# Fifteen small loads queued behind the last store of a biased softmax

## The chip, the cores and the metric

The kernel runs on one core of one Trainium2 chip. The metric is the device time of one execution in microseconds (us), as the median over runs; the profile's span is the time from the first to the last instruction of one profiled execution.

## What is computed

For logits of shape (2, 8, 2112, 2112) and a table of 33 bias values for each of 8 heads, each logit gets the bias of its relative position, clipped to 16 on both sides, and each row of 2112 then goes through a softmax:

```python
rel = pos[:, None] - pos[None, :]
rel_clipped = np.clip(rel, -16, 16) + 16
logits = logits + rel_bias[:, rel_clipped][None]
exp = np.exp(logits - logits.max(axis=-1, keepdims=True))
return exp / exp.sum(axis=-1, keepdims=True)
```

All of it is in fp32. 285 MB are read and 285 MB written.

## The kernel before

The 33,792 rows are dealt to the 128 partitions, 264 consecutive rows (`ROWS`) to each. They are worked on in 44 chunks of 6 rows in each partition (`R`, `N`), in four buffers `X0` to `X3` of 50,688 bytes in each partition (`NBUF`). A chunk is loaded whole (128 partitions x 6 rows, 6,336 KB), changed in place and stored from the same buffer.

The order of the work is written out by hand, with semaphores and without a planner:

- SP issues every load and store of `X`. `load` (line 78) loads a chunk and counts on `ld[b]`; `store` (line 82) waits until DVE has scaled the rows and counts on `st[b]`. The first chunk is loaded as six single rows (line 88). Then a loop (line 204) stores a chunk, waits until an older store has landed, and loads the next chunk into that buffer. After the loop the last chunks are stored without further loads; the very last one goes out as two halves of three rows.
- `take` (line 74) makes an engine wait until a semaphore has reached a number and subtracts it again. SP's program ends with four of these, one for each buffer's stores.
- ACT loads the bias table once, to all partitions (line 97), and does the exponentials with their row sums (line 175).
- DVE builds a strip of bias values from the table in its first microseconds, and then copies it (line 160), adds it to the logits with the row's extremum (line 166), takes reciprocals of the sums (line 183), and scales the rows (line 187).
- GpSimd makes two small tables of indices.

Of the kernel before, what the change touches and what calls it, by code (L numbers as in the profile page):

```python
# [7 lines left out]
FP32 = mybir.dt.float32  # L8
# [7 lines left out]
def kernel(  # L16
# [6 lines left out]
    nc = tc.nc  # L23
    P = 128
# [3 lines left out]
    W = 2 * MR + 1  # L28
# [13 lines left out]
    io = ctx.enter_context(tc.tile_pool(name="io", bufs=1))  # L42
# [4 lines left out]
    tot = io.tile([P, STEP], FP32, tag="tot", name="tot")  # L47
    rec = io.tile([P, STEP], FP32, tag="rec", name="rec")
    ip = io.tile([P, 3, PB], I32, tag="ip", name="ip")
    ps = ctx.enter_context(tc.tile_pool(name="ps", bufs=1, space=bass.MemoryType.PSUM))  # L50
    M = ps.tile([P, 4096], FP32, tag="M", name="M")

    def view(t, offset, dims):

        return bass.AP(tensor=t.tensor, offset=t.offset + offset, ap=[[list(t.ap[0])[0], P]] + dims)

    def rows(t, j, n):

        return bass.AP(tensor=t.tensor, offset=t.offset + j * S, ap=[[ROWS * S, P], [1, n * S]])

    with tc.tile_critical(no_gpsimd_drain=True):
# [6 lines left out]
        rb = nc.alloc_semaphore("rb")  # L68
        pre = nc.alloc_semaphore("pre")
        idx = nc.alloc_semaphore("idx")  # L70
        dve = nc.alloc_semaphore("dve")

        def take(eng, sem, n):
            eng.wait_ge(sem, n).then_inc(sem, -n)  # L74
# [5 lines left out]
        def store(j, b, s0=0, n=R):  # L80
            take(nc.sync, scaled, n)
            nc.sync.dma_start(
                out=rows(out, j + s0, n), in_=X[b][:, s0 * S : (s0 + n) * S]
            ).then_inc(st[b], 16)


        for r in range(R):
            nc.sync.dma_start(
                out=X[0][:, r * S : (r + 1) * S], in_=rows(logits, r, 1)
            ).then_inc(ld[0] if r == R - 1 else pre, 16)  # L90
        for n in range(1, NBUF):
# [6 lines left out]
            out=rbB,  # L98
            in_=bass.AP(tensor=rel_bias.tensor, offset=rel_bias.offset, ap=[[0, P], [1, H * W]]),
# [27 lines left out]
        for m, op in ((eq, ALU.is_equal), (gt, ALU.is_gt), (le, ALU.is_le), (lt, ALU.is_lt)):  # L127
# [4 lines left out]
            out=view(F, 0, [[W, H], [1, W]]), in0=view(F, 0, [[W, H], [1, W]]),  # L132
# [9 lines left out]
            out=view(F, 0, [[W, PB], [1, W]]), in0=view(F, SC + 2 * PB, [[1, PB], [0, W]]),  # L142
# [7 lines left out]
            out=view(M, U, [[ROWS, PB], [1, W]]), in0=view(F, 0, [[W, PB], [1, W]]),  # L150
            in1=view(F, SC + 8 * PB, [[1, PB], [0, W]]), op=ALU.add))
        then(v.tensor_copy(out=view(M, U + W, [[ROWS, PB], [1, ROWS - W]]),  # L152
                           in_=view(F, SC + 7 * PB, [[1, PB], [0, ROWS - W]])))
# [56 lines left out]
            store(n * R, n % NBUF)  # L210
        store((N - 1) * R, (N - 1) % NBUF, 0, HALF)
        store((N - 1) * R, (N - 1) % NBUF, HALF, R - HALF)
        for b in range(NBUF):
            take(nc.sync, st[b], 32 if b == (N - 1) % NBUF else 16)

# [29 lines left out]
```

## Time and profile before

| what | us |
|---|---|
| time, median of 3 runs (1330.96 to 1332.85) | 1331.0 |
| span of the profiled execution | 1327.7 |
| time of the median outside the span | 3.3 |
| DVE busy | 976.6 |
| ACT busy | 575.2 |
| one load of a chunk, from issue to landing (median) | 44.6 |
| one store of a chunk, from issue to landing (median) | 52.6 |

The profiled execution's own time outside its span isn't recorded apart, so the span is set against the median of the runs. In the page, DVE is the vector engine, ACT the scalar engine, POOL is GpSimd, and SP the sync engine, which here only issues DMAs and waits. A `q` behind an engine's name stands for its sequencer. "DMA" in a window is the mean busy share of the core's 16 DMA engines; q1 is the queue that SP issues on and q10 the one that ACT issues on. Instructions that only issue a DMA or wait aren't counted as busy.

### The profile page before, as it was taken

The numbers are of one execution on the slowest core, as the hardware profiler recorded it, in microseconds if no ns is written. First come the engines' busy times: TensorE is split into PE (matmuls) and PEld (weight loads), VectorE is DVE, ScalarE is ACT, GpSimd is POOL, SyncE is SP. The second block draws the span as 40 slices with busy tenths as digits, with TensorE's granted clock in tenths as the row PEclk, the third lists the DMA queues.
The fourth block names the chain that finished last, engine by engine and source line by source line (L and its number), as shares of the span: only waits on it lengthen the run. The fifth ranks groups of instructions, "written<-read, shape, count | busy, mean of one in ns | idle before, by whom it ended". The sixth has DMA issues, their size and how long they took to land. (4 is left out here: it accounts for less than half of the span.)

```text
span 1327.7 us, 2454 instructions
## 1 busy us (share of the span) xinstructions
DVE 976.6 (74%) x911; ACT 575.2 (43%) x539; POOL 0.4 (0%) x6
## 2 busy tenths in 40 slices
DVE  6999667777777776687778777677877776687772
ACT  2564333444444343345444333444444343335440
POOL 0000000000000000000000000000000000000000
DMA  9999999999999999999999999999999999999998
GB/s 392 431 428 437 435 420 437 435 434 425 435 437 434 428 435 434 435 429 429 438 438 432 426 438 437 437 425 437 437 437 425 435 440 437 428 432 438 437 426 359
DMA packets 13683, 571.11 MB, mean 430 GB/s; under 512 B 1521, under 2 KB 1649, under 8 KB 1649
## 3 DMA queue, kind: packets, MB, share of 16 engines
q1 hardware_dynamic: 13536, 570.96, 99.6%
q10 hardware_dynamic: 144, 0.14, 0.1%
q14 instruction: 3, 0.02, 0.0%
HBM read 285.61 MB, written 285.47 MB: 430 GB/s over the span
## 5 line engine op out<-in xcount | busy, mean ns | idle before, releaser
L166 DVE CUSTOM_DVE_ANT_0 X<-X,F 128x2112 f32<-128x2112 f32 x264 | 605.2, 2354 | 301.3 <-DVEq L74 301.3
L175 ACT ACTIVATE X<-X,nmax 128x2112 f32<-128x2112 f32 x264 | 541.7, 2052 | 539.3 <-ACTq L74 517.6
L187 DVE TENSOR_SCALAR X<-X,rec 128x2112 f32<-128x2112 f32 x264 | 332.4, 1315 | 13.2
L175 ACT ACT_TABLE_LOAD x11 | 14.1, 1283 | 183.3 <-ACTq L74 183.3
L175 ACT ACTIVATION_READ_ACCUMULATOR X<-X,nmax 128x1 f32 x264 | 49.2, 186 | 0.0
L160 DVE COPY F<-M 128x2135 f32 x11 | 26.1, 2374 | 6.3 <-DVEq L74 6.3
L166 DVE DVE_READ_ACCUMULATOR2_ANT nmax<- 128x1 f32 x264 | 21.7, 82 | 0.0
L183 DVE RECIPROCAL rec<-tot 128x3 f32<-128x3 f32 x88 | 14.9, 170 | 0.0
L131 DVE TENSOR_TENSOR F<-F 128x264 f32<-128x264 f32 x1 | 0.4, 434 | 4.7 <-DMA F<-in_rel_bias_dram 4.7
L152 DVE COPY M<-F 128x1848 f32<-128x1848 f32 x1 | 2.1, 2077 | 0.0
L118 DVE TENSOR_SCALAR ip<-ip 128x8 int32<-128x8 int32 x1 | 0.2, 173 | 1.3 <-POOL ip L102 1.3
L135 DVE TENSOR_REDUCE rbS<-F 128x33 f32<-128x264 f32 x1 | 0.6, 610 | 0.0
L149 DVE TENSOR_TENSOR M<-F 128x264 f32<-128x264 f32 x1 | 0.4, 441 | 0.0
L141 DVE TENSOR_TENSOR F<-F,rbS 128x264 f32<-128x264 f32 x1 | 0.4, 425 | 0.0
L128 DVE TENSOR_SCALAR F<-F 128x8 f32<-128x8 f32 x4 | 0.4, 166 | 0.0
L154 DVE COPY M<-rbS 128x247 f32<-128x247 f32 x1 | 0.4, 408 | 0.0
L139 DVE TENSOR_SCALAR F<-F,rbS 128x8 f32<-128x8 f32 x1 | 0.2, 231 | 0.0
L145 DVE SCALAR_TENSOR_TENSOR F<-F,rbS 128x8 f32<-128x8 f32 x1 | 0.2, 225 | 0.0
L140 DVE TENSOR_SCALAR F<-F,rbS 128x8 f32<-128x8 f32 x1 | 0.2, 222 | 0.0
L146 DVE SCALAR_TENSOR_TENSOR F<-F,rbS 128x8 f32<-128x8 f32 x1 | 0.2, 219 | 0.0
L124 DVE TENSOR_TENSOR F<-ip 128x8 f32<-128x8 int32 x1 | 0.2, 167 | 0.0
L121 DVE TENSOR_TENSOR F<-ip 128x8 f32<-128x8 int32 x1 | 0.2, 166 | 0.0
(9 smaller groups left out, 1.2 us busy)
## 6 DMA issues: line engine op xcount, KB each, us to landing
X<-in_logits_dram SPq DMA_DIRECT2D x43, 6336.0 KB, 44.6
out_dram<-X SPq DMA_DIRECT2D x43, 6336.0 KB, 52.6
X<-in_logits_dram SPq DMA_DIRECT2D x6, 1056.0 KB, 12.1
out_dram<-X SPq DMA_DIRECT2D x2, 3168.0 KB, 21.1
F<-in_rel_bias_dram ACTq DMA_DIRECT2D x1, 132.0 KB, 6.2
```

The source lines that it names most:

```text
L128: then(v.tensor_scalar(out=m, in0=dp, scalar1=0.0, scalar2=None, op0=op))
L131: then(v.tensor_tensor(out=view(F, 0, [[W, H], [1, W]]), in0=view(F, 0, [[W, H], [1, W]]), in1=view(F, SC + 3 * PB, [[1, H], [0, W]]), op= ...
L135: then(v.tensor_reduce(out=rbS[:, :], in_=view(F, 0, [[1, W], [W, H]]), axis=mybir.AxisListType.X, op=ALU.add))
L141: then(v.tensor_tensor(out=view(F, 0, [[W, PB], [1, W]]), in0=view(F, SC + 2 * PB, [[1, PB], [0, W]]), in1=view(rbS, W - 1, [[0, PB], [-1, ...
L149: then(v.tensor_tensor(out=view(M, U, [[ROWS, PB], [1, W]]), in0=view(F, 0, [[W, PB], [1, W]]), in1=view(F, SC + 8 * PB, [[1, PB], [0, W]] ...
L152: then(v.tensor_copy(out=view(M, U + W, [[ROWS, PB], [1, ROWS - W]]), in_=view(F, SC + 7 * PB, [[1, PB], [0, ROWS - W]])))
L154: then(v.tensor_copy(out=M[:, 0:U], in_=low.to_broadcast([P, U])))
L160: v.tensor_copy(out=F[:, :], in_=M[:, bass.ds(ROWS - STEP - j, FW)]).then_inc(dve, 1)
L166: v.tensor_tensor_reduce(out=x, in0=x, in1=F[:, STEP - 1 - r : STEP - 1 - r + S], scale=-1.0, scalar=BIG, op0=ALU.add, op1=ALU.min, accum_ ...
L175: nc.scalar.activation(out=x, in_=x, func=EXP, scale=-1.0, bias=nmax[:, r : r + 1], accum_out=tot[:, r : r + 1],).then_inc(expd, 1)
L183: v.reciprocal(out=rec[:, r0 : r0 + HALF], in_=tot[:, r0 : r0 + HALF]).then_inc(inv, 1)
L187: v.tensor_scalar_mul(out=x, in0=x, scalar1=rec[:, r : r + 1]).then_inc(scaled, 1)
```

## The change

Behind the last store SP issues 15 loads from the bias table into a new tile `mark`, which nothing reads. Load k (from 15 down to 1) goes into k partitions, with k + 1 floats in each, from rows that lie 16 floats apart in the table; the place in the tile is another one for each k. All count on one new semaphore `mk`, and SP waits for all 15 before it waits for the stores.

```diff
+    mark = io.tile([P, 160], FP32, tag="mark", name="mark")
...
+        mk = nc.alloc_semaphore("mk")
...
         store((N - 1) * R, (N - 1) % NBUF, 0, HALF)
         store((N - 1) * R, (N - 1) % NBUF, HALF, R - HALF)
+        for k in range(15, 0, -1):
+            nc.sync.dma_start(
+                out=bass.AP(tensor=mark.tensor, offset=mark.offset + k * (k + 1) // 2, ap=[[list(mark.ap[0])[0], k], [1, k + 1]]),
+                in_=bass.AP(tensor=rel_bias.tensor, offset=rel_bias.offset, ap=[[W // 2, k], [1, k + 1]]),
+            ).then_inc(mk, 16)
+        take(nc.sync, mk, 16 * 15)
         for b in range(NBUF):
             take(nc.sync, st[b], 32 if b == (N - 1) % NBUF else 16)
```

## The prediction

> **What bounds the kernel now.** I read the page's first three parts, then the chain that ended last, then the windows of the last microseconds, then the instructions of SP's queue. The page says that the DMA engines bind the kernel from end to end.
>
> ```profile
> span 1327.7 us, 2454 instructions
> DVE 976.6 (74%) x911; ACT 575.2 (43%) x539; POOL 0.4 (0%) x6
> DMA  9999999999999999999999999999999999999998
> q1 hardware_dynamic: 13536, 570.96, 99.6%
> HBM read 285.61 MB, written 285.47 MB: 430 GB/s over the span
> ```
>
> The busiest compute engine, DVE, is idle a quarter of the span, while one queue, q1 (SP's, which carries every load and store of X), keeps the 16 engines busy for 99.6% of it. So the body of the kernel is set by the bytes of X, and the change leaves those alone. Everything that it adds comes after the last store in SP's program. The only place to look at is therefore the tail. The chain that ended last finishes on the last two scalings, and the windows show what follows them.
>
> ```profile
> 1301.05 2.54 DVE X L187 x2
> core 0: us, DVE busy (x) ACT busy (x) POOL busy (x), PEclk, DMA share, GB/s
> 1319.00:1320.00 1.00, 0.00 (x0) 0.00 (x0) 0.00 (x0) 1.00 1.06 456
> 1320.00:1321.00 1.00, 0.00 (x0) 0.00 (x0) 0.00 (x0) 1.00 0.53 228
> 1321.00:1322.00 1.00, 0.00 (x0) 0.00 (x0) 0.00 (x0) 1.00 0.47 203
> 1323.00:1324.00 1.00, 0.00 (x0) 0.00 (x0) 0.00 (x0) 1.00 0.41 177
> 1324.00:1325.00 1.00, 0.00 (x0) 0.00 (x0) 0.00 (x0) 1.00 0.18 76
> 1325.00:1326.00 1.00, 0.00 (x0) 0.00 (x0) 0.00 (x0) 1.00 0.12 51
> 1326.00:1327.00 1.00, 0.00 (x0) 0.00 (x0) 0.00 (x0) 1.00 0.00 0
> ```
>
> Compute ends at 1301.05 + 2.54 = 1303.59 us. The rings are full until 1320; then the share falls to 0.53 and on to 0.41 of 16 engines. About nine engines are through with their part of the last store by 1321, about seven run on, and two of them until 1326. The end is thus set by the latest engine, not by all of them. SP's own records tell when the program notices.
>
> ```profile
> 1299.67 4.34 SPq L82 DMA_DIRECT2D out_dram<-X  x2
> L74 SPq EVENT_SEMAPHORE  x5: 17/17/17, 1303.6 to 1326.6; - x5
> out_dram<-X SPq DMA_DIRECT2D x2, 3168.0 KB, 21.1
> ```
>
> The two half stores are issued between 1299.67 and 1304.01, and SP's last wait (line 74, the helper that waits and subtracts) passes at 1326.6. From 1304.01 to 1326.6, 22.6 us, SP does nothing but wait. What lies behind 1326.6 is 1.1 us of closing the program, which stays. The median of the runs is 1331.0, 3.3 us above this span; I take those 3.3 us as unchanged too.
>
> **The change, part by part.** Nothing is removed, and nothing ahead of the last store is moved: the loads, stores and waits of DVE, ACT and POOL stand as they did, and the new tile is the last of its pool, so that no other tile gets another place. Added are 15 load instructions on SP, their packets, and one wait ahead of the four old ones.
>
> *Issuing.* SP issues 15 DMAs behind the last store, with no waits between them. No DMA into fewer than 128 partitions stands in the trace, so I take the price of other issues:
>
> ```profile
> 0.97 3.34 SPq L88 DMA_DIRECT2D X<-in_logits_dram  x6
> 4.36 1.74 SPq L78 DMA_DIRECT2D X<-in_logits_dram  x3
> L88 SPq DMA_DIRECT2D X<-in_logits_dram x6: 388/488/707, 1.0 to 3.7; - x6
> L82 SPq DMA_DIRECT2D out_dram<-X x45: 332/339/363, 43.1 to 1303.7; - x45
> ```
>
> At the start, nine loads go out back to back in 3.34 + 1.74 us, 0.56 us each; a lone store takes 0.339 us, and the dearest issue of these rows is 0.707 us. Fifteen of them take 5.1 us (15 x 0.339) to 10.6 us (15 x 0.707), and 8.5 us at 0.56. SP is therefore done at 1304.01 + 8.5 = 1312.5, and at 1314.6 in the dear case: 6 to 8 us before the early engines end (about 1321), and 12 to 14 before the late ones do. I cost the issue at nothing; what covers it is the last store itself, still in its rings. The cover is gone only if an issue costs more than 22.6 / 15 = 1.5 us. Behind the waiting SP nothing is queued but the four store waits, and no other engine waits for SP until the program closes.
>
> *Packets.* Load k goes into k partitions, so it is 120 rows in all, each of 8 to 64 bytes, plus a completion from each DMA engine used. Every DMA of before leaves one such small packet per engine, as the window of the very end shows:
>
> ```profile
> DMA packets 2, 0.00 MB, mean 0 GB/s; under 512 B 2, under 2 KB 2, under 8 KB 2
> q1 hardware_dynamic: 2, 0.00, 0.7%
> q10 hardware_dynamic: 144, 0.14, 7.2%
> ```
>
> The first two rows are of the window 1326.08 to 1326.24, in which the two last completions run: 0.7% of 16 engines x 160 ns is 18 ns, or 9 ns for each. The third row is of the window 0 to 10 us: the bias table's load of before (128 rows of 1,056 bytes and 16 completions), 7.2% of 16 x 10 us = 11.5 us, or 80 ns for each packet among heavy traffic. A mark of one row and one completion on an engine is thus between 2 x 9 = 18 ns and 80 + 9 = 89 ns. Its row of 8 to 64 bytes is nearer in size to the 4-byte completion than to 1,056 bytes, so I take 25 ns. What counts is how many marks lie on the engine that finishes last. If load k uses k engines and always the same first ones, that is any number from 0 to 15, and the trace doesn't name its engines; I take the middle, 7.5. That gives 7.5 x 25 ns = 0.19 us, with ends of 0 and 15 x 89 ns = 1.3 us.
>
> The Trainium skill (DMA: Bandwidth & Descriptors, Why a DMA increments its semaphore by 16 and not by 1) says that such a DMA runs on the largest count up to 16 that divides the outer dimensions, on the lowest-numbered engines. By it engine 0 carries 15 marks and engine 15 none, so the sum goes from 0 to 1.3 us with the number of the late engine; no row here shows a DMA on fewer than 16.
>
> *The first read behind a store.* Whether a small load behind a store on the same ring shows a read's delay isn't in the trace for an empty ring. Downwards the bound is nothing: in the whole middle, loads follow stores in the same rings at a share of 9 tenths or more. Upwards it is the start of the program, where the rings were idle:
>
> ```profile
> GB/s 0 0 0 0 0 0 0 13 30 253 182 241 76 84 177 300 228 241 325 161 275 325 245 439 254 444 439 372 473 406 406 372 507 439 372 439 372 541 406 372
> F<-in_rel_bias_dram ACTq DMA_DIRECT2D x1, 132.0 KB, 6.2
> X<-in_logits_dram SPq DMA_DIRECT2D x43, 6336.0 KB, 44.6
> ```
>
> In slices of 0.25 us, the first load, issued at 0.97, moves in bulk from the tenth slice on, at 2.25 us: 1.3 us. The bias load landed after 6.2 us, in the crowd of the first loads. In the tail the marks are queued 8 us or more before the late engines come to them, and the case is nearer to the middle than to the start, so I take 0, and keep 1.3 and 6.2 for a rival.
>
> *SP's waits.* Before, three of the four store waits had passed when the last one did. Now the wait for the marks stands ahead of all four, so where the marks land last, four more waits run behind the end. The row of line 74 has 17 ns for one. What lies between two of them I bound by the pair of register instructions that SP runs ahead of each load, whose starts read 0.1 us apart:
>
> ```profile
> L78 SPq FUSED_REGOPS  x40: 46/46/46, 81.0 to 1236.9; - x40
> L78 SPq MOVE X<-in_logits_dram x40: 29/29/29, 81.1 to 1237.0; - x40
> ```
>
> So four cost 0.07 us (4 x 17 ns) to 0.4 us (4 x 0.1); I take 0.3, since a sequencer step with its own fetch is nearer to the second.
>
> *Sum.* 0 + 0.19 + 0 + 0.3 = 0.5 us: the span goes to 1328.2 and the time to 1331.0 + 0.5 = 1331.5. Without a rival the ends are +0 and 1.3 + 0.4 = +1.7 us.
>
> **The rivals.**
>
> *One read's delay behind the store.* The late engine begins a mark's read only when its store is out. Then one trip is added to the 0.5: 1.3 us gives 1332.8, 6.2 us gives 1337.7. For it: the late engines run alone at the end, and with no further bytes to move nothing hides a delay. Against it: rings full of queued work showed none. It passes my line of 0.2% (2.7 us, about what a measurement of this kernel can tell from no change) when the trip takes over 2.2 us, roughly even odds between its ends.
>
> *Every mark pays its own trip (slower).* If an engine doesn't start a mark until the one before has completed, the engine with all 15 pays 15 x 1.3 = 19.5 us. If it is an early engine (stores out at 1321) that ends at 1340.5, 13.9 us behind 1326.6, a time of 1345; if the latest, at 1331.0 + 19.5 = 1350.5. It decides from (1326.6 - 1321) / 15 = 0.37 us for a mark on an early engine. For it: nothing but small DMAs one behind the other is anywhere in the trace. Against it: the packets above are 9 and 80 ns apart in cost, and the DMA share stays at 1.06 in 1319 to 1320 although completions of the half stores lie in those rings. The Trainium skill (DMA: Bandwidth & Descriptors, Anatomy of one DMA) speaks for it: a fixed part of some 2 us for each DMA, most of it waiting for the write's receipt. Paid by each mark in turn that would be an estimated 30 us, paid once an estimated 2; the middle of this trace, with a load and a store every 30 us at full share, shows no such gap.
>
> *SP is held up.* If no more than nine DMAs may be under way (the most that the trace shows issued back to back), the last store's landing must come before the rest are issued. Three stores are open at 1304, so six marks go, two more as the two earlier stores land, and seven are left for 1326.6: 7 x 0.56 + 1.3 to 6.2 of landing is 5.2 to 10.1 us, a time of 1336.2 to 1341.1. For it: issue at the start rose from 388 to 707 ns as the queue filled. Against it: those nine had 128 rows each, and a mark has 15 at most.
>
> *The marks don't do anything.* If the late engine carries no mark, the new wait passes before the store's, and the time stays at 1331.0. That lies within the forecast.
>
> **How the numbers follow.** The forecast (+0 to +1.7 us) has 0.56; one trip 0.20, half of it below 2.7 us; every mark its trip 0.12; SP held up 0.08; and 0.04 is left for a gain, for which no row has a reason, since the same bytes go through the same rings. Within 0.2%: 0.56 + 0.10 = 0.66. Slower: 0.10 + 0.12 + 0.08 = 0.30. Faster: 0.04. The likeliest case's own time is 1331.5. The range goes from 1330.5, half a microsecond under the lowest of the three runs (1330.96), to 1337, which takes in nearly all of the single trip and leaves out the trip of every mark, most of SP's hold-up and the gain, 0.2 in all.
>
> **What would show it.** In the changed profile SP should show 15 new issues after 1304 with the last ended by 1315; q1 should have 120 + 120 more packets; the DMA share to 1326 should read as before; and SP's last wait should pass at 1326.7 to 1328.3. New issues above 1.5 us or a pause among them would show the third rival. Small packets that run on after 1327 with tenths of a microsecond between them would show the second, and one gap of over 1 us ahead of the first small packet on the late engines the first. The forecast is wrong if SP's last wait is over 2.7 us later than 1326.6 with the body unchanged, or if the body itself, up to 1304, changes its length.

## The result and the profile after

| | median us | runs | range us |
|---|---|---|---|
| before | 1330.8 | 21 | 1329.12 to 1332.85 |
| changed | 1332.24 | 21 | 1330.59 to 1334.23 |

The ratio is 1.0013, with a 95% interval of 1.0007 to 1.0018: 1.4 us slower by the medians, a small loss that is clear of noise and lies within the 0.2% of the forecast. The page of the changed kernel shows the body as it was, and 240 more packets on q1.

```profile
span 1328.8 us, 2470 instructions
DVE 976.6 (73%) x911; ACT 575.2 (43%) x539; POOL 0.4 (0%) x6
q1 hardware_dynamic: 13776, 570.96, 99.5%
```

DVE and ACT do what they did, to the tenth of a microsecond. The span is 1.1 us longer. Each run of the changed kernel lies 1.7 to 1.9 us above its span (the profiled one: 1330.59 and 1328.8), so the 3.3 us that stood between the span and the median of before were not all time outside the program: the profiled execution was also one of the shorter ones. The tail is read from SP. First its issues in the changed kernel, then the record of the last half store (line 84; it was line 82), then SP's last waits (line 76; it was 74) in three windows: all from 1315 on, those from 1326.9 to 1327.0, and those from 1327.45 to 1327.7.

```profile
1299.17 4.34 SPq L84 DMA_DIRECT2D out_dram<-X  x2
1303.56 14.96 SPq L216 DMA_DIRECT2D mark<-in_rel_bias_dram  x15
...
L216 SPq DMA_DIRECT2D mark<-in_rel_bias_dram x15: 344/1000/1063, 1303.6 to 1318.2; - x15
...
L84 SPq DMA_DIRECT2D out_dram<-X x1: 332/332/332, 1303.2 to 1303.2; - x1
DMA to landing us min/median/max: 22.9/22.9/22.9
...
L76 SPq EVENT_SEMAPHORE  x5: 17/17/17, 1327.0 to 1327.7; - x5
L76 SPq EVENT_SEMAPHORE  x1: 17/17/17, 1327.0 to 1327.0; - x1
L76 SPq EVENT_SEMAPHORE  x3: 17/17/17, 1327.5 to 1327.7; - x3
```

The same two rows in the profile of before:

```profile
L82 SPq DMA_DIRECT2D out_dram<-X x1: 332/332/332, 1303.7 to 1303.7; - x1
DMA to landing us min/median/max: 22.9/22.9/22.9
```

The last half store lands 22.9 us after its issue in both, so the marks behind it don't slow it. In the changed kernel it lands at 1303.2 + 22.9 = 1326.1; the wait for the marks passes at 1327.0, and the last of the four store waits at 1327.7. The marks are thus 0.9 us late, SP's own waits add 0.7, and that execution lost 1.6 us. Its span is only 1.1 us longer, because its last store was issued 0.5 us earlier than in the profile of before.

Where do the 0.9 us come from? A completion is here the packet of 4 bytes with which a DMA is counted as done on one of its engines, and a ring is the line of DMAs that one engine works off for one queue. The marks' sizes tell one engine's packets from another's: in the window of 1324.28 to 1324.46 one engine works off the completion of its store and then marks of 64 bytes, 60 bytes, and so on.

```profile
DMA  0001101110111011011011011011101110100000
DMA packets 23, 0.00 MB, mean 3 GB/s; under 512 B 23, under 2 KB 23, under 8 KB 23
```

23 packets are one completion of the store and 11 marks with two packets each. They take 0.14 us in all, 13 ns for a mark, so they run as cheaply as the forecast had it. But they are not done then. The trace's record of the semaphores has that engine's store counted at 1324.83 and the last marks at 1326.19, 1326.37, 1326.56, 1326.75 and 1326.94: one every 0.19 us, and 1324.83 + 11 x 0.19 = 1326.92. The engine that ends last, with its store counted at 1326.04, carries no mark. These 0.9 us belong to this execution; two profiles below show that they change with the order in which the engines end.

### The profile page after: what moved, and what is told of

It is laid out like the page before. It is cut to its first block, busy times and chain, and to the rows that moved or that the text cites. A ratio compares the mean times of both kernels' runs of the same rounds, so it can differ in the third digit from the quotient of the medians.

```text
span 1328.8 us, 2470 instructions
## 1 busy us (share of the span) xinstructions
DVE 976.6 (73%) x911; ACT 575.2 (43%) x539; POOL 0.4 (0%) x6
```

## The experiments

Theory A, formed from these records: on one engine's ring the completions of DMAs follow one another by 0.18 to 0.19 us, each; an engine with n marks is done n times that after its store. Rival B: one read trip, whatever the number. Rival C: only SP's additional waits cost. Times are compared with runs of the kernel before on the same chip.

**Fifteen on every engine.**

```diff
-        for k in range(15, 0, -1):
-            ...  # k partitions, k + 1 floats
+        for k in range(15):
+            ...  # out=mark[0:16, 10 * k : 10 * k + 10], 16 partitions, 10 floats
```

> 15 loads, each of 10 floats into 16 partitions, so that every engine carries 15 marks, the latest one too. Theory A: the wait for the marks passes 15 x 0.19 = 2.9 us after the last store has landed, and the time is 2.9 + 0.7 = 3.6 us over the kernel before, 1334.4. Rival B: 1 to 2 us over it, as in the changed kernel. Rival C: 0.7 us over it. An issue takes 0.34 us instead of the 1.0 us of the changed kernel if the price belongs to a count of engines other than 16, and 1.0 us if it belongs to small rows.

Measured: 1333.91 against 1330.9, ratio 1.0023 (1.0014 to 1.0032), 3.0 us. The last half store and SP's last waits:

```profile
L84 SPq DMA_DIRECT2D out_dram<-X x1: 332/332/332, 1304.4 to 1304.4; - x1
DMA to landing us min/median/max: 22.9/22.9/22.9
...
L76 SPq EVENT_SEMAPHORE  x5: 17/17/17, 1329.8 to 1330.6; - x5
```

From 1304.4 + 22.9 = 1327.3 to 1329.8 is 2.5 us, 0.17 us for each of 15, and 0.8 us of SP's waits follow. The loss is 3.3 us in the profile, near A's 3.6. C's 0.7 is out; B's 2 us lies still inside the time's interval (1.9 to 4.3 us). An issue took 0.75 us, neither of the two values expected.

**Forty-five on every engine.**

```diff
-        for k in range(15, 0, -1):
+        for k in range(45):
+            ...  # out=F[0:16, 16 * k : 16 * k + 10]; F is no longer read by then
-        take(nc.sync, mk, 16 * 15)
+        take(nc.sync, mk, 16 * 45)
```

> 45 loads of 10 floats into 16 partitions (into a tile that is no longer read), three times the marks on every engine. Theory A: 45 x 0.19 = 8.6 us and 0.7 us of waits over the kernel before, 1340.1; the distance to the kernel with 15 such loads is 30 x 0.19 = 5.7 us. Rival B: 1 to 2 us over the kernel before, no more than with 15. Packets alone (22 to 26 ns for a mark): 45 x 0.025 + 0.7 = 1.8 us over it, and 0.8 us from the kernel with 15.

Measured: 1339.31, ratio 1.0067 (1.0053 to 1.0081), 8.4 us; 5.4 us from the kernel with 15, or 0.18 us for each of the 30 more. B and a price of packets alone are out.

```profile
1305.35 27.94 SPq L216 DMA_DIRECT2D F<-in_rel_bias_dram  x45
...
L84 SPq DMA_DIRECT2D out_dram<-X x1: 333/333/333, 1305.0 to 1305.0; - x1
...
L76 SPq EVENT_SEMAPHORE  x5: 17/17/17, 1335.9 to 1336.2; - x5
```

The last half store lands at 1305.0 + 22.9 = 1327.9 here, as its own row says too; from there to 1335.9 are 8.0 us, 0.18 for each mark. One reservation: SP was issuing until 1333.3, so its issues were not far from setting the end themselves.

**All on one engine.**

```diff
-                out=...,  # k partitions
+                out=...,  # 1 partition, k + 1 floats
```

> 15 loads, each into one partition, so that all 15 marks lie on one engine, by the changed kernel's sizes one that ends early (1320.6 us). Theory A: its marks are done 15 x 0.19 = 2.9 us later, at 1323.5, ahead of the last store's landing near 1326; the wait for the marks passes before the store's and the time is that of before, 1330.8 (up to 0.2 over it). Rival B: the same. A third way, in which the marks' landing waits for every engine's store, gives 1 us and more over it. Issues take 0.34 us each, as the last one (one partition) did in the changed kernel.

Measured: 1329.94, ratio 0.9996 (0.9987 to 1.0005): no difference. SP's waits in the windows 1323 to 1324 and 1326 to 1328:

```profile
L76 SPq EVENT_SEMAPHORE  x2: 17/17/17, 1323.7 to 1323.8; - x2
L76 SPq EVENT_SEMAPHORE  x1: 17/17/17, 1327.0 to 1327.0; - x1
```

The marks pass at 1323.7 and the last store at 1327.0. Their 15 counts stand in the record at 1321.135, 1321.317, 1321.498 and so on to 1323.677, 0.181 to 0.183 us apart, 0.1815 on average, although all had been issued by 1312.3. This is the cleanest view of the pace, and it costs nothing on an engine that ends early. The issues took 0.47 us, not 0.34.

**One load with 45 small rows for each engine.**

```diff
-        for k in range(15, 0, -1):
-            ...
-        take(nc.sync, mk, 16 * 15)
+        nc.sync.dma_start(
+            out=bass.AP(..., ap=[[..., 16], [16, 45], [1, 10]]), in_=...,
+        ).then_inc(mk, 16)
+        take(nc.sync, mk, 16 * 1)
```

> One load in place of 45, with the same 45 rows of 10 floats for each of 16 partitions: as many small rows on every engine, and one completion instead of 45. If the 0.18 us belongs to the completion of a DMA, the wait for it passes about 0.2 us behind the last store's landing and the time is 0.5 us (0.2 to 1.0) over the kernel before, near 1331.5. If it belongs to each small row, 45 x 0.18 = 8 us stay and the time is 1339.3.

Measured: 1330.17 against 1330.14, ratio 1.0 (0.9991 to 1.001).

```profile
q1 hardware_dynamic: 14272, 570.98, 99.6%
...
F<-in_rel_bias_dram SPq DMA_DIRECT2D x1, 28.1 KB, 22.8
...
L84 SPq DMA_DIRECT2D out_dram<-X x1: 332/332/332, 1303.7 to 1303.7; - x1
...
L76 SPq EVENT_SEMAPHORE  x5: 17/17/17, 1326.9 to 1327.2; - x5
```

736 more packets than before (14272 - 13536) and no time: the load's wait passes at 1326.9, 0.3 us behind the store (1303.7 + 22.9 = 1326.6). So the 0.18 us belongs to each DMA's completion on an engine, not to a row or a packet, and rival B's trip is at most 0.3 us.

**The wait for the marks behind the store waits.**

```diff
-        take(nc.sync, mk, 16 * 15)
         for b in range(NBUF):
             take(nc.sync, st[b], 32 if b == (N - 1) % NBUF else 16)
+        take(nc.sync, mk, 16 * 15)
```

> The wait for the marks is moved behind the four store waits; nothing else changes. Theory A (each mark's completion on one engine follows the one before by about 0.19 us, so that an engine with n marks is done n x 0.19 us after its store, and SP's four waits run behind that): the store waits then pass during the wait for the late engines, 0.7 us of waits behind the end fall to under 0.1, and the time comes 0.5 to 0.7 us under the changed kernel's 1332.2, near 1331.6. Rival B (one read trip of 1 to 2 us behind the last store, whatever the number of marks): the same saving. Rival C (only SP's waits cost): all of the loss goes, 1330.8.

Measured: 1332.28, ratio 1.0012 (1.0003 to 1.0021), no less than the changed kernel. In its profile the two last waits, for the last store and for the marks, pass in the same tenth, right behind the store's landing (window 1328 to 1330).

```profile
L76 SPq EVENT_SEMAPHORE  x2: 17/17/17, 1328.2 to 1328.2; - x2
```

The interval is 2.4 us wide and the expected saving 0.6, so the time decides nothing, and the expected saving was not seen. The profile doesn't decide either, because the marks weren't late in it: the record of the semaphores has their last count at 1327.65, 0.5 us ahead of the last store's at 1328.15, where the same marks came 0.9 us behind it in the profile of the changed kernel. The engine that ends last carries no mark in either; what differs is how long before it the engines with many marks end. So the loss is not the same in each execution, and how the 1.4 us of the medians divide between late marks and SP's waits isn't shown.

**Where SP stops.**

```diff
-        for k in range(15, 0, -1):
+        for k in range(13, 0, -1):
+            ...  # 8 - k % 2 partitions
-        take(nc.sync, mk, 16 * 15)
+        take(nc.sync, mk, 16 * 13)
```

> 13 loads, in turn into 7 and into 8 partitions, in place of 15. Two questions of SP's own. First, a stop of 0.46 us stood behind the 17th instruction after the last store in each kernel with marks, whatever that instruction was. If it belongs to the place in the program, it now stands behind the third store wait instead of the first (13 loads, the marks' wait and three store waits make 17); if it belongs to the wait for a certain buffer, it stays behind the first. Second, the issue: if a count of engines other than 16 and 1 costs more, 8 and 7 alike take 0.9 to 1.0 us; if only counts that are no power of two do, 8 takes 0.75 us and 7 takes 1.0.

This is one run, so its time is not compared. Three waits of this kernel in the window 1327.4 to 1327.8 follow the marks' wait at once, and the last one stands alone in 1328.1 to 1328.3:

```profile
L76 SPq EVENT_SEMAPHORE  x4: 17/17/17, 1327.5 to 1327.7; - x4
L76 SPq EVENT_SEMAPHORE  x1: 17/17/17, 1328.2 to 1328.2; - x1
```

The stop of 0.46 us has moved from behind the first store wait to behind the third: it belongs to a place in the program, the 17th instruction behind the last store. With 45 marks SP pauses for 0.43 us between its 17th and its 18th mark. Before the change SP's program ended short of this place. What happens there stays open. Loads into 7 and into 8 partitions both took a median of 1.04 us to issue: in this run a power of two makes no difference. The marks are late by more than in the changed kernel: their wait passes at 1327.5, 1.9 us behind the last store (issued at 1302.65, landed 22.9 us later).

**The marks ahead of the half stores.**

```diff
+        for k in range(15, 0, -1):
+            ...
         store((N - 1) * R, (N - 1) % NBUF, 0, HALF)
         store((N - 1) * R, (N - 1) % NBUF, HALF, R - HALF)
-        for k in range(15, 0, -1):
-            ...
```

> The same 15 loads, issued ahead of the two half stores in SP's idle 25 us, and waited for at the same place. Theory A (completions in series on a ring, behind whatever store is in front of them): they stand behind an older store, are done long before the end, and the time is that of before, 1330.9 (within 0.3 us). If what costs is that the marks exist at all (more packets, more instructions), the time stays at 1332.2.

Measured: 1332.47 against 1331.18, ratio 1.0009 (1.0 to 1.0018). The interval begins at no loss, so the time alone doesn't say that it cost anything. The profile does: the last half store now lands 24.3 us after its issue. Theory A as stated expected the time of before; it left out what stands behind the marks.

```profile
L84 SPq DMA_DIRECT2D out_dram<-X x1: 367/367/367, 1305.8 to 1305.8; - x1
DMA to landing us min/median/max: 24.3/24.3/24.3
```

1.4 us more than in any kernel above. In the packet records the first store packets of 25,344 bytes behind the marks took up to 2.14 us, where the others take 0.94. One profile could still be chance, so the next kernel enlarges the effect.

**Thirty on every engine ahead of the half stores.**

```diff
+        for k in range(30):
+            ...  # out=mark[0:16, 5 * k : 5 * k + 5]
         store((N - 1) * R, (N - 1) % NBUF, 0, HALF)
         store((N - 1) * R, (N - 1) % NBUF, HALF, R - HALF)
-        for k in range(15, 0, -1):
-            ...
-        take(nc.sync, mk, 16 * 15)
+        take(nc.sync, mk, 16 * 30)
```

> 30 loads of 5 floats into 16 partitions, issued ahead of the two half stores in SP's idle 25 us. The kernel with 15 marks at that place had first store packets behind its marks that took up to 2.1 us instead of 0.94. Amended theory A (completions in series hold up whatever is behind them in the same ring): every engine is held for 30 x 0.18 = 5.4 us ahead of the half stores, less what it would have been idle, and the time is 4 to 5.5 us over the kernel before, near 1336. Rival (the marks are free as long as they are done before the end, and that kernel's slower runs were chance): the time is that of before, within 0.5 us.

Measured: 1336.26 against 1331.23, ratio 1.0041 (1.0028 to 1.0055): 5.0 us.

```profile
L84 SPq DMA_DIRECT2D out_dram<-X x2: 658/2805/4952, 1301.4 to 1305.4; - x2
DMA to landing us min/median/max: 24.2/26.0/27.8
```

The last half store, issued at 1305.4, takes 4.95 us to issue instead of 0.33 and lands 27.8 us on instead of 22.9, 4.9 us more. SP's slow issue isn't what does it: the first half store, issued in 0.66 us, lands 24.2 us on, where it took 19.4 in the profile of before, 4.8 us more; in the row of before's stores (line 82) it is the shortest:

```profile
DMA to landing us min/median/max: 19.4/52.6/53.9
```

So completions in series hold the ring for whatever comes next, and here SP was held up at its issue as well.

**The marks on another queue.**

```diff
-            nc.sync.dma_start(
+            nc.scalar.dma_start(
```

> The same 15 loads at the same place of the program, but issued on ACT's queue, which has no stores in it and whose last work ends near 1298; SP still waits for them ahead of the stores. Theory A: they need not wait for the last store in the ring, land by 1315, and the time is that of before, 1330.9. If the new small packets cost wherever they are queued, the time is 1332.2.

Measured: 1331.09 against 1331.18, ratio 0.9999 (0.999 to 1.0008). The time is as expected, the way there only partly: issued from 1298.9 on, the marks weren't done by 1315. Their wait passed at 1328.8, and the last store's at 1329.7:

```profile
L216 ACTq DMA_DIRECT2D mark<-in_rel_bias_dram x15: 600/788/1599, 1298.9 to 1310.7; - x15
...
L76 SPq EVENT_SEMAPHORE  x5: 17/17/17, 1328.8 to 1329.7; - x5
```

Their packets, on q10, run from 1303.0 to 1328.4 beside those of the stores on q1, and end just ahead of them. That the time is that of before is thus shown; that marks on another queue land early is not.

**Two that decided nothing.** Both are changed from the kernel with 45 marks on every engine: the source on the chip instead of in HBM, and rows of 1,056 bytes.

```diff
-                in_=bass.AP(tensor=rel_bias.tensor, ...),  # 45 loads of 40 bytes a row
+                in_=rbS[0:16, 0:10],                       # the one
+                in_=bass.AP(..., ap=[[0, 16], [1, H * W]]) # the other, out in 16 rows of F
```

> 45 loads as in the kernel with 45, but from the on-chip copy of the table instead of from HBM. If the 0.18 us for each completion is the round trip of the write and its count, it stays: 8.0 us between the last store's landing and the marks' wait, 1339.3. If it is the read from HBM, it falls to well under 0.1 us, 4 us at most, 1335 or less.

> 45 loads of 1,056 bytes a row (into 16 partitions) instead of 40. The packet of such a row takes 45 to 80 ns by the bias load of before. If completions in series set the pace, the row hides under them: 0.18 us each, 1339.3. If the pace is the sum of row and completion, it becomes 0.18 + 0.04 = 0.22 us and more, 10 us in all, 1341.

Measured: 1347.45 (ratio 1.0111, 1.0093 to 1.0129) and 1339.38 (1.0056, 1.0041 to 1.0072). SP's issues of the first, with its waits, and of the second:

```profile
1306.43 38.35 SPq L216 DMA_DIRECT2D F<-rbS  x45
...
L76 SPq EVENT_SEMAPHORE  x5: 17/17/17, 1345.9 to 1346.2; - x5
```

```profile
1305.79 30.04 SPq L216 DMA_DIRECT2D F<-in_rel_bias_dram  x45
...
L76 SPq EVENT_SEMAPHORE  x5: 17/17/17, 1337.1 to 1337.4; - x5
```

In the first, SP issues until 1344.8, and in the second until 1335.8, each 1.1 to 1.3 us ahead of the wait; a mark of these kernels lands no sooner than 1.7 us after its issue began. The issue, not the completions, ended them, so neither says what the 0.18 us consists of. That stays open.

## Why the prediction was right

The forecast held: 1332.24 lies in the range, and the loss of 0.13% within the 0.2% given 0.66. Its +0.5 us was a third of the 1.4 measured. By its own steps:

- *The body.* Unchanged, as said; the last half store lands 22.9 us after its issue in both.
- *Issuing.* Sized at 0.56 us each with an end at 1312.5, and 1314.6 in the dear case; it took 1.0 us each and ended at 1318.5, past the 1315 that was named as a sign. The cover, given as 1.5 us for each, was still there. No row of before had such a price: loads into 2 to 15 partitions took 0.92 to 1.06 us in the changed kernel and 0.75 to 1.02 in the one with its wait moved, loads into 16 about 0.75, and loads into one 0.25 to 0.56. With 45 marks the issue fell from 0.77 to 0.42 us once most of the stores had left the rings, near 1322.
- *Packets.* This is the term that was mis-sized. A mark's packets took 13 ns, under the 25 assumed, but what counts is its completion, 0.18 to 0.19 us. The 9 ns of the completion's packet were read as its price. In the profile of the changed kernel the engine that decided carried 11 marks, not 7.5: 11 x 0.19 gave 2.1 us behind a store that ended 1.2 us ahead of the last, 0.9 us in all against 0.19.
- *The first read.* 0 was right: one load with 45 rows on every engine passed 0.3 us behind the store, and cost nothing that could be measured.
- *SP's waits.* 0.3 was right for the four waits themselves: with 45 marks they pass from 1335.9 to 1336.2. In the changed kernel they took 0.7, because a stop of 0.46 us, brought before the end by the new length of the program, fell among them.

That the loss stayed so small was in part luck. The price of a mark was wrong by a factor of about seven, and what kept it cheap is that the engines with many marks happened to end early enough: the marks came 0.9 us behind the last store in the changed kernel, 0.5 us ahead of it in the one with its wait moved, and 1.9 us behind it with 13 marks on 7 or 8 engines. With 15 on every engine the loss was 3.0 us, more than the 2.7 us of the 0.2%.

Of the rivals, the one in which every mark pays in turn had the mechanism right and the price wrong: 0.18 us, not 1.3. It named 0.37 us for a mark as the point from which an early engine with 15 marks decides; at 0.18 that engine was done at 1323.7 of 1327.0, which the kernel with all marks on one engine shows. The sign named for it, small packets that run on after 1327 with tenths of a microsecond between them, would have missed it: the last small packet of the changed kernel starts at 1325.7, and only the counts of the semaphore are 0.19 us apart. The evidence held against it, that the DMA share shows no gap behind a completion, was weak: in the profile of before every packet of 25,344 bytes takes 0.94 to 0.95 us, also behind a completion, so one completion doesn't show ahead of a large packet. That the packet hides the 0.18 us is an inference. The Trainium skill (DMA: Bandwidth & Descriptors, Anatomy of one DMA) gives a fixed part of some 2 us for a DMA, in a section on DMAs that GpSimd issues, while SP issues these. The runs show 1.7 us as the soonest landing of a mark, but 0.18 us as the pace of marks queued one behind the other. Its rule on the count of engines (the same page, Why a DMA increments its semaphore by 16 and not by 1) agrees with the trace: the marks' sizes show every number of marks from 0 to 15 on an engine. Which numbers the engines have, the trace doesn't tell.

SP held up, the third rival, didn't happen with 15 marks. With 30 marks ahead of two half stores it did: one issue took 4.95 us.

## What to carry to other kernels

A DMA behind others in a ring costs its completion even where its bytes cost nothing: here 0.18 us for each DMA on each engine that it uses, in series. Whether the kernel pays it hangs on which engine ends last. Many tiny loads are best made one load with many rows (45 rows in one DMA: no loss; 45 DMAs: 8.4 us), or put on a queue without the critical stores (here no loss), or on engines that end early (here no loss). A small packet's length in the trace is not its price; look at when its semaphore is counted, and at the time of the packet behind it.

## What was not expected of the hardware

- Completions in series: 0.1815 us apart on one engine with one-partition loads, 0.17 to 0.19 us elsewhere, while the packets themselves stand 13 ns apart. What the 0.18 us consists of stays open.
- A ring full of completions lengthens the next packet: 2.14 us at the most behind up to 15 marks, and 4.0 to 5.2 us for sixteen packets behind 30, for a packet that else takes 0.94 us.
- SP stops for 0.46 us at one place of its program (behind the 17th instruction after the last store): between two of SP's waits in the five kernels with 13 or 15 marks there, and between two marks in the one with 45, for 0.43 us.
- The last half store lands 22.9 us after its issue in every kernel that has nothing new ahead of it, while the moment of its issue wanders between 1302.7 and 1306.0 us.
